# A decoder layer on one core: softmax joining in PSUM, weightings by table, filler transposes, new places

## The chip, the cores and the metric

The kernel runs on one core of one Trainium2 chip. The metric is device time in microseconds, from runs of the whole program; lower is better. The engines are TensorE (PE, with its weight loads PEld), VectorE (DVE), ScalarE (ACT), GpSimd (POOL) and SyncE (SP, which here issues most DMAs).

## The reference

One decoder layer over 1024 tokens of width 1024, in float32. The normalised input goes through one projection into 256 pooling channels and queries, keys and values for 12 heads of 64. Attention is evaluated under three (window, dilation) settings, merged by their softmax denominators.

```python
DILATED_CONFIGS = ((128, 1), (512, 4), (2048, 16))
def dilated_attention(q, k, v):
    for window, dilation in DILATED_CONFIGS:
        o, lse = dilated_branch(q, k, v, window, dilation)   # banded softmax; lse = m + log(den)
        ...
    w = softmax(stack(lses), axis=0)
    return sum(w[..., None] * stack(outs), axis=0)
...
h = rms_norm(x, ln_pre_mix); proj = h @ w_in
mix = concat([pool_out, attn_out]) @ w_out
x = x + rms_norm(mix, ln_post_mix)
h = rms_norm(x, ln_pre_ffn)
f = (silu(h @ w_gate) * (h @ w_up)) @ w_down
x = x + rms_norm(f, ln_post_ffn)
```

## The kernel before, in words

Each float32 product is three passes of TensorE: operands are split into a high part (ACT copies it) and a low part (DVE or POOL subtracts), and high x high, high x low and low x high are summed in PSUM. `wtile` loads a weight tile through the SP queue and splits it (line 245 is ACT's copy, line 249 the subtraction on POOL or DVE). `PRM['we']` says for each of the 12 query and key weight tiles whether DVE (1) or POOL (0) subtracts.

Attention is worked in 12 units, numbered 0 to 11. A unit is a pair of heads and a half of the tokens: pairs 0 to 3 with both halves, then pairs 4 and 5 in the first half (units 8 and 9) and in the second (10 and 11). A unit has five sorts of steps:

- `scores`: products of queries and keys into a bank of tag s; DVE adds the mask and takes the extremum (line 678), ACT takes the exponential and its sum (line 681). The result `pp` is not yet normalised. There are two sides: natural order and strided by four, which together cover the three settings.
- `merge`: the two sides' extrema and sums (`sx`) are joined into one weight per row, `wv`. Two small products (`ex` with a selector) bring the other side's numbers into a bank `e` of tag s; then some small steps follow on DVE, and one exponential on ACT: `em` (line 703), a reduction (704), the minimum `nm` (708), the difference `dd` (710), its exponential (711), `de` (713), the sum (714), the reciprocal (715) and `wv` (717).
- `weigh`: 16 pieces of `pp`, of 128 x 256 or 128 x 128, are multiplied by `wv` in place, by DVE (line 731) or POOL (line 733). One list `wd` of 16 entries says which, the same for all units. Pieces 0 to 3 are those of the first group.
- `values`, turning: groups of three or four blocks of `pp` are transposed through TensorE (line 197) into a bank of tag t; ACT copies the high part (778), DVE subtracts the low part (779), giving `ptr`.
- `values`, products: `ptr` times the values into a bank of tag o.

Beside these run the projections of the next pairs: rope on queries and keys (`rope`, whose two later steps at lines 453 and 456 are on POOL), and value rows. These projections are the "fill": lists of single products, cut into pieces, one piece to a unit.

Every step has a place on a common axis, in units, from `PRM`: `own` gives places for a single unit (`s0`, `s1` first and last score step, `m` merge, `w0`, `w1` weightings, `t0`, `t1` turnings, `v0`, `v1` products), `vt` the loads of values, `lr` and `lc` the loads of the mix for the output projection. `emit` sorts all steps by place and issues them; TensorE keeps the order in which its instructions are issued. Before a step that would wait, `await_` may pull products of the fill ahead: as many as the planner's own clock (0.235 us a product) says are needed before a due time, and `PRM["x"]` adds a number of further pulls for single steps. A negative number there takes the due time back by as many pulls.

After attention come the output projection, a norm, and the feed-forward part in blocks (a Strassen-like scheme of seven products instead of eight: `seven`, with sums of blocks at lines 1346 to 1352 on DVE, splits at 1380 and 1382 on ACT and POOL). `c0`, `c1` and `c2` hold the places of the norm's steps, squares and block sums in the passage from the one to the other, `ew` those of two weight loads.

Of the kernel before, what the change touches and what calls it, by code (L numbers as in the profile page):

```python
# [8 lines left out]
F32 = mybir.dt.float32  # L9
# [26 lines left out]
 'we': (1, 1, 1, 0, 0, 0, 0, 0, 0, 0, 1, 1),  # L36
 'nt0': 0.4926,
 'nt1': 0.628,
# [111 lines left out]
 'cut': 5,  # L150
 'ew': (0.2207, 0.1793),
 'c1': (0.1405, 0.1771, 0.2651, 0.7788, 0.6483, 1.0204, 1.4605, 1.6658, 0.9644, 0.8869),
 'c2': ((1.0107, 1.1787), (1.1914, 1.4876)),
 'e0': ((0.26, 0), (0.42, 0), (0.47, 0.9)),
 'ea': (0, 2, 4),
 'e1': (1.12, 1.25, 1.8, 1.2, 1.5)}
PRM["x"] = {(0, 'm'): 5, (0, 's', 0): 8, (0, 's', 1): 6, (0, 's', 2): 5, (0, 's', 3): 3, (0, 's', 4): 2, (0, 's', 6): 3,
# [31 lines left out]
def hybrid_block(ctx: ExitStack, tc: tile.TileContext, xT, w_in, w_v, w_pin, w_pool, w_out, w_gate, w_up, w_down,  # L189
# [27 lines left out]
    def bank(tag):  # L217
        return psum.tile([P, 512], F32, name="ps_" + tag, tag=tag)
# [226 lines left out]
    def eng(name):  # L445
        return [(nc.vector if b else nc.gpsimd) for b in PRM[name]]
# [107 lines left out]
    def new_q(pr, h):  # L554
        pr.q[h] = qkp.tile([P, 2, 512], F32R, name="qh", tag="qh", bufs=QB), qlow[len(taken) % 2]
        taken.append((pr.p, h))
        return pr.q[h]

    def q_half(pr, h):
        return proj_half(2 * pr.p, h, pr.st, lambda ps: rope(ps, h, new_q(pr, h), False, eng("rq")))  # L560

    def k_half(pr, h):
        def done(ps):
            if h == 0:
                pr.k = qkp.tile([P, 2, T], F32R, name="k", tag="k", bufs=2)
            did(("k", pr.p, h))
            rope(ps, h, pr.k, True, eng("rk"))
        return proj_half(2 * pr.p + 1, h, pr.st, done)
# [117 lines left out]
    def merge(pr, h):  # L686
# [20 lines left out]
        nm = small.tile([P, 16], F32, name="nm", tag="nm", bufs=1)  # L707
        nc.vector.tensor_tensor(nm, sv[:, 0, :, 0], sv[:, 1, :, 0], ALU.min)
        dd = small.tile([P, 2, 16], F32, name="dd", tag="dd", bufs=1)
        nc.vector.tensor_tensor(dd, nm[:, None].to_broadcast([P, 2, 16]), sv[:, :, :, 0], ALU.subtract)  # L710
# [3 lines left out]
        nc.vector.tensor_tensor(nm, de[:, 0], de[:, 1], ALU.add)
        nc.vector.reciprocal(nm, nm)
        wv = small.tile([P, 2, 4, 2], F32, name="wv", tag="wv")
        nc.vector.tensor_tensor(wv.rearrange("p s j a -> p (s j a)"), nm, dd[:, 0], ALU.mult)  # L717
# [4 lines left out]
    def weigh(pr, h):  # L722
        un = pr.un[h]

        def step(hd, side, j):
            un.wv
            did(("w", pr.p, h, hd, side))
            lo = 128 if narrow(side, h, j) else 0
            pv = un.pp[hd, side][:, j, lo:]
            if PRM["wd"][hd * 8 + (1 - side) * 4 + j]:  # L730
                nc.vector.tensor_scalar(pv, pv, un.wv[:, side, j, hd:hd + 1], None, op0=ALU.mult)
            else:
                nc.gpsimd.tensor_scalar(pv, pv, un.wv[:, side, j, hd:hd + 1], 1.0, op0=ALU.mult, op1=ALU.mult)  # L733
        return [lambda a=(hd, side, j): step(*a) for hd in range(2) for side in (1, 0) for j in range(4)]
# [26 lines left out]
    def values(pr, h):  # L761
# [5 lines left out]
        def turn(hd, gi):  # L767
# [187 lines left out]
    def put(steps, lo, hi):  # L955
        plan.append((steps, lo, hi))
# [833 lines left out]
```

## Time and profile before

| | |
|---|---|
| median of 3 runs | 1144.0 us (1143.02 to 1144.89) |
| profiled execution | 1144.5 us, span 1142.7 us |
| PE busy | 1126.4 us, 99% |
| DVE, ACT, POOL busy | 784.2, 545.3, 601.6 us |
| mean granted clock of PE | 0.997 |

In the profile's rows a time is that from the span's start, then the duration (of a run of like instructions, from the first's start to the last's end), the engine, the line of the kernel, the operation and the tiles. In brackets stands the idle time before it and the instruction that ended it. A line is often a helper's: line 194 is every product, line 197 every transpose.

### The profile page before, as it was taken

How to read it: one execution, taken by the hardware profiler on the slowest of the kernel's cores; microseconds unless marked ns; L12 is line 12 of the kernel's file. 1: busy time of each engine (PE TensorE's matmuls, PEld its weight loads, DVE VectorE, ACT ScalarE, POOL GpSimd, SP SyncE). 2: the span in 40 equal slices, each digit the busy share in tenths (PEclk: the TensorE clock that was granted, in tenths of full speed). 3: DMA queues.
4: the chain of work that ended last, by engine and by line, in shares of the span. 5: the costliest groups of instructions: out<-in, count | busy, mean ns of one | idle time of the engine just before them, and what ended most of it. 6: DMA issues, size and time to landing. Idle time of an engine off the chain costs nothing.

```text
span 1142.7 us, 17021 instructions
## 1 busy us (share of the span) xinstructions
PE 1126.4 (99%) x6050; PEld 976.5 (85%) x6050; DVE 784.2 (69%) x1463; ACT 545.3 (48%) x1035; POOL 601.6 (53%) x541
## 2 busy tenths in 40 slices
PE   9999999999999999999999999999999999999997
PEld 7999899999898888888788888888888888888887
DVE  7957878787898676979557655666566375464594
ACT  7446676666676665855333222322232435343431
POOL 0102646465576222241587556876675977656531
PEclk9999999999999999999999999999999999999999
DMA  8324151514136557530343354445445869766642
GB/s 286 114 79 167 56 167 57 166 57 166 57 111 225 187 203 272 184 111 28 129 175 141 127 195 174 166 175 196 173 149 191 286 207 364 230 206 200 203 166 73
DMA packets 85076, 189.02 MB, mean 165 GB/s; under 512 B 8704, under 2 KB 23552, under 8 KB 83584
## 3 DMA queue, kind: packets, MB, share of 16 engines
q1 hardware_dynamic: 84704, 187.68, 46.7%
q8 instruction: 47, 0.77, 0.3%
q14 instruction: 37, 0.30, 0.1%
q10 hardware_dynamic: 288, 0.27, 0.1%
HBM read 134.96 MB, written 52.95 MB: 164 GB/s over the span
## 4 chain that ended last, share of the span: by engine, by line
PE 83%; DVE 7%; POOL 3%; issue 3%; ACT 2%; DMA 1%; SPq 0%; DVEq 0%; POOLq 0%; ACTq 0%
PE ps_pj L194 29%; PE ps_o L194 22%; PE ps_s L194 21%; PE ps_t L194 7%; PE ps_t L197 3%; ACT pp L681 1%; DVE pp L678 1%; DVE sq L1137 1%; POOL fw L1382 1%; POOL whl L1382 1%; DMA xraw<-in_xT_dram 1%; POOL whl L249 0%; DVE z L1169 0%; DVE ql L484 0%; DMA rw<-in_w_up_dram 0%
## 5 line engine op out<-in xcount | busy, mean ns | idle before, releaser
L194 PE MATMUL ps_pj<-x,whl 128*128 128x512 f32 x480 | 141.7, 407 | 0.0
L1382 POOL TENSOR_TENSOR fw<-rw,fw 128x512 fp32r<-128x512 f32 x74 | 101.1, 1390 | 63.2 <-ACT fw L1380 61.8
L249 POOL TENSOR_TENSOR whl<-wraw,whl 128x512 fp32r<-128x512 f32 x50 | 66.4, 1348 | 110.3 <-ACT whl L245 110.2
L194 PE MATMUL ps_o<-tT,fw 128*128 128x512 f32 x504 | 119.4, 393 | 1.8 <-DVE p L1417 1.8
L194 PEld LDWEIGHTS ps_o<-tT,fw 128*128 128x128 f32 x504 | 95.5, 190 | 22.2 <-DVE p L1417 2.2
L733 POOL TENSOR_SCALAR pp<-pp,wv 128x256 f32<-128x256 f32 (+1 forms) x156 | 71.8, 480 | 80.1 <-DVE wv L717 71.4
L681 ACT ACTIVATE pp<-pp,sx 128x128 f32<-128x128 f32 (+1 forms) x192 | 89.4, 468 | 35.0 <-DVE sx L678 34.1
L1382 POOL TENSOR_TENSOR whl<-rw,whl 128x512 fp32r<-128x512 f32 x42 | 59.4, 1438 | 66.8 <-ACT whl L1380 66.8
L194 PEld LDWEIGHTS ps_pj<-x,whl 128*128 128x128 f32 x480 | 84.9, 189 | 9.2
L1380 ACT ACTIVATE fw<-rw 128x1024 fp32r<-128x1024 f32 x37 | 38.5, 1056 | 94.5 <-DVE rw L1348 41.3
L194 PE MATMUL ps_pj<-whl,x 128*128 128x256 f32 x528 | 80.9, 293 | 0.0
L1529 POOL TENSOR_TENSOR op<-rw,op 128x512 fp32r<-128x512 f32 x38 | 60.4, 1588 | 36.3 <-ACT op L1528 36.2
L1528 ACT ACTIVATE op<-rw 128x1024 fp32r<-128x1024 f32 x38 | 40.2, 1060 | 65.9 <-DMA rw<-bd 25.5
L194 PEld LDWEIGHTS ps_pj<-whl,x 128*128 128x128 f32 x528 | 70.3, 196 | 0.1
L779 DVE TENSOR_TENSOR ptr<-ps_t,ptr 128x512 fp32r<-128x512 f32 (+1 forms) x84 | 55.8, 665 | 14.3 <-ACT ptr L778 13.9
L194 PE MATMUL ps_pj<-b,fw 128*128 128x512 f32 x264 | 61.6, 389 | 0.0
L453 POOL TENSOR_TENSOR rsw<-rsw,sinr 128x512 f32<-128x512 f32 x20 | 26.3, 1317 | 66.4 <-DVE rsw L451 66.4
L194 PE MATMUL ps_o<-ptr,v 128*128 128x128 f32 (+1 forms) x472 | 56.5, 254 | 1.9 <-DVE ptr L779 1.2
L194 PEld LDWEIGHTS ps_pj<-b,fw 128*128 128x128 f32 x264 | 49.5, 188 | 10.3
L778 ACT ACTIVATE ptr<-ps_t 128x512 fp32r<-128x512 f32 (+1 forms) x84 | 48.4, 576 | 20.3 <-PE ps_t L197 18.9
L194 PEld LDWEIGHTS ps_o<-ptr,v 128*128 128x128 f32 x472 | 52.6, 163 | 5.7 <-DVE ptr L779 1.6
L194 PE MATMUL ps_s<-k,qh 128*128 128x128 f32 (+1 forms) x192 | 53.7, 291 | 0.0
(318 smaller groups left out, 2897.9 us busy)
## 6 DMA issues: line engine op xcount, KB each, us to landing
rw<-bd SPq DMA_DIRECT2D x77, 256.0 KB, 4.5
v<-vd SPq DMA_DIRECT2D x22, 512.0 KB, 4.8
rw<-wsd SPq DMA_DIRECT2D x44, 256.0 KB, 3.9
rw<-in_w_gate_dram SPq DMA_DIRECT2D x20, 512.0 KB, 3.7
rw<-in_w_up_dram SPq DMA_DIRECT2D x20, 512.0 KB, 4.6
bd<-p SPq DMA_DIRECT2D x33, 256.0 KB, 3.0
rw<-in_w_down_dram SPq DMA_DIRECT2D x33, 256.0 KB, 4.3
fw<-in_w_down_dram SPq DMA_DIRECT2D x16, 512.0 KB, 4.1
```

Source lines behind the costliest of these rows:

```text
L194: return tc.keep_in_program_order(nc.tensor.matmul(*a, **k))
L197: return tc.keep_in_program_order(nc.tensor.transpose(dst, src, by))
L249: parts.append(eng.tensor_tensor(dst[:, 1, at:at + w], src[:, at:at + w], dst[:, 0, at:at + w].bitcast(F32), ALU.subtract))
L453: pin(eng[0].tensor_tensor(s, s, sinr[:, sl], ALU.mult))
L681: nc.scalar.activation(pt[:, j, lo:], pt[:, j, lo:], AF.Exp, bias=sx[:, 0, side, j, hd, 0:1], scale=-1.0, accum_out=sx[:, 0, side, j, hd, ...
L733: nc.gpsimd.tensor_scalar(pv, pv, un.wv[:, side, j, hd:hd + 1], 1.0, op0=ALU.mult, op1=ALU.mult)
L778: nc.scalar.activation(ptr[:, 0, :w], t[:, :w], AF.Copy)
L779: nc.vector.tensor_tensor(ptr[:, 1, :w], t[:, :w], ptr[:, 0, :w].bitcast(F32), ALU.subtract)
L1380: nc.scalar.activation(w[n][:, :, 0], raw[n], AF.Copy)
L1382: low[0] = nc.gpsimd.tensor_tensor(w[n][:, i, 1], raw[n][:, i], w[n][:, i, 0].bitcast(F32), ALU.subtract)
L1528: nc.scalar.activation(w[:, :, 0], raw, AF.Copy)
L1529: nc.gpsimd.tensor_tensor(w[:, 0, 1], raw[:, 0], w[:, 0, 0].bitcast(F32), ALU.subtract)
```

## The change

- `merge`: `nm` and `dd` are put into the free columns of the PSUM bank `e` instead of SBUF; the minimum and the sum become reductions over two rows; the sum and reciprocal go into a new small tile `ns`.
- `weigh`: a table `wu`, by unit and piece, overrides `wd`; the value 2 is ACT, as a copy scaled by the column of `wv`.
- `turn`: a table `dm`, by unit and group, gives a number of transposes of the identity into the group's bank ahead of its own; it holds one entry, 18 for group 0 of unit 9.
- `eng`: a table `ro` overrides the engines of a rope step; one of its ten entries differs from the default (pair 2's key, second half, addition on DVE).
- the fill's borders between units are moved by `fb`, in threes of products.
- `we`: other weight tiles are split on DVE.
- places (`own`, `vt`, `lr`, `lc`, `c0`, `c1`, `c2` and others) and the numbers of further pulls (`x`) are changed.

```diff
- 'we': (1, 1, 1, 0, 0, 0, 0, 0, 0, 0, 1, 1),
+ 'we': (0, 0, 0, 1, 1, 0, 0, 1, 0, 1, 0, 1),
- 'lw': (4.153, 0.453),
+ 'lw': (4.665, 0.499),
...
          9: {'s0': -0.058,
-             't1': 1.7709,
+             't1': 1.7717,
              'v1': 2.0469,
-             'w1': 1.052,
-             'w0': 0.6506,
-             'v0': 1.2034,
-             's1': 0.464,
-             't0': 0.9223,
-             'm': 0.6239},
+             'w1': 1.0264,
+             'w0': 0.6547,
+             'v0': 1.1793,
+             's1': 0.4719,
+             't0': 0.8982,
+             'm': 0.6222},
...
          6: {'s1': 0.3673,
...
+             'w1': 1.2338,
+             's0': -0.0707,
+             'w0': 0.6079,
+             't0': 0.8477},
...
- 'c0': (0.0502, 0.0986, 0.2259, 0.595, 0.2709, 0.6103, -0.3497, 0.3883, 0.2606, 0.1296),
+ 'c0': (0.0502, 0.0986, 0.2259, 0.595, 0.2709, 0.6103, -0.3497, 0.3883, 0.1363, 0.1661),
- 'ew': (0.2207, 0.1793),
- 'c1': (0.1405, 0.1771, 0.2651, 0.7788, 0.6483, 1.0204, 1.4605, 1.6658, 0.9644, 0.8869),
- 'c2': ((1.0107, 1.1787), (1.1914, 1.4876)),
+ 'ew': (0.2363, 0.1483),
+ 'c1': (0.1405, 0.1771, 0.2651, 0.7788, 0.5274, 0.9613, 1.4605, 1.6658, 0.9644, 0.9565),
+ 'c2': ((1.0107, 1.1699), (1.1914, 1.6904)),
...
+ 'wu': {(8, 7): 1, (6, 10): 2, ...  (9, 1): 2, (9, 6): 2, (9, 7): 2, (9, 9): 2, (7, 0): 2, (7, 1): 2, (7, 7): 2, ...
+        (4, 2): 2, (4, 3): 2, (4, 4): 2, (4, 11): 2, (4, 12): 2, (4, 14): 2, (4, 15): 2, ...},
+ 'dm': {(9, 0): 18},
+ 'fb': (1, 0, 0, 0, 0, 0, 1, -1, 0),
+ 'ro': {..., ('rk', (2, 1)): (0, 1), ...}}
...
-    def eng(name):
-        return [(nc.vector if b else nc.gpsimd) for b in PRM[name]]
+    def eng(name, key=None):
+        return [(nc.vector if b else nc.gpsimd) for b in G["ro"].get((name, key), G[name])]
...
-        nm = small.tile([P, 16], F32, name="nm", tag="nm", bufs=1)
-        nc.vector.tensor_tensor(nm, sv[:, 0, :, 0], sv[:, 1, :, 0], ALU.min)
-        dd = small.tile([P, 2, 16], F32, name="dd", tag="dd", bufs=1)
+        nm, dd = e[:, 128:144], e[:, 160:192].rearrange("p (o n) -> p o n", o=2)
+        de = small.tile([P, 64], F32, name="de", tag="de", bufs=1)[:, :32].rearrange("p (o n) -> p o n", o=2)
+        ns = small.tile([P, 16], F32, name="ns", tag="ns", bufs=1)
+        nc.vector.tensor_reduce(nm, sv[:, :, :, 0].rearrange("p o n -> p n o"), op=ALU.min, axis=mybir.AxisListType.X)
         nc.vector.tensor_tensor(dd, nm[:, None].to_broadcast([P, 2, 16]), sv[:, :, :, 0], ALU.subtract)
         nc.scalar.activation(dd, dd, AF.Exp)
-        de = small.tile([P, 2, 16], F32, name="de", tag="de", bufs=1)
         nc.vector.tensor_tensor(de, dd, sv[:, :, :, 1], ALU.mult)
-        nc.vector.tensor_tensor(nm, de[:, 0], de[:, 1], ALU.add)
-        nc.vector.reciprocal(nm, nm)
+        nc.vector.tensor_reduce(ns, de.rearrange("p o n -> p n o"), op=ALU.add, axis=mybir.AxisListType.X)
+        nc.vector.reciprocal(ns, ns)
         wv = small.tile([P, 2, 4, 2], F32, name="wv", tag="wv")
-        nc.vector.tensor_tensor(wv.rearrange("p s j a -> p (s j a)"), nm, dd[:, 0], ALU.mult)
+        nc.vector.tensor_tensor(wv.rearrange("p s j a -> p (s j a)"), ns, dd[:, 0], ALU.mult)
...
-            if PRM["wd"][hd * 8 + (1 - side) * 4 + j]:
+            n = hd * 8 + (1 - side) * 4 + j
+            e = G["wu"].get((unit_of[pr.p, h], n), G["wd"][n])
+            if e == 2:
+                nc.scalar.activation(pv, pv, AF.Copy, scale=un.wv[:, side, j, hd:hd + 1])
+            elif e:
                 nc.vector.tensor_scalar(pv, pv, un.wv[:, side, j, hd:hd + 1], None, op0=ALU.mult)
...
             t = bank("t")
+            for n in range(G["dm"].get((unit_of[pr.p, h], hd * len(groups) + gi), 0)):
+                turned_to(t[:, :P], idt, idt)
...
+    seq, ends_at = [x for fs in fill for f in fs for x in f], [0]
     for u in range(1, 11):
-        put(Fill([x for f in fill[u] for x in f]).by(3), u + (G["f0"] if u > 1 else -0.07), u + (0.25 if u == 10 else 1) + G["f1"])
+        ends_at.append(sum(len(f) for fs in fill[:u + 1] for f in fs) + (3 * G["fb"][u - 1] if u < 10 else 0))
+    for u in range(1, 11):
+        put(Fill(seq[ends_at[u - 1]:ends_at[u]]).by(3), u + (G["f0"] if u > 1 else -0.07), u + (0.25 if u == 10 else 1) + G["f1"])
```

More of the change, by code (lines that the diff above doesn't have):

```diff
@@ L35 @@
  'sqa': (1, 0, 0, 1, 0, 0, 0, 1),
- 'we': (1, 1, 1, 0, 0, 0, 0, 0, 0, 0, 1, 1),
- 'nt0': 0.4926,
- 'nt1': 0.628,
+ 'we': (0, 0, 0, 1, 1, 0, 0, 1, 0, 1, 0, 1),
+ 'nt0': 0.5548,
+ 'nt1': 0.5715,
  'oq': (0, 1, 1, 1, 0, 0, 0, 1),
@@ L41 @@
  'fl': 12,
[2 rows of a table removed]
+ 'lt': 2.711,
+ 'ls': 2.296,
  'lm': 2.745,
[4 rows of a table removed]
+ 'lw': (4.665, 0.499),
+ 'nm': 0.1243,
+ 'n2': -0.0696,
+ 'n0': 0.1888,
  'n1': 0.223,
@@ L71 @@
         'u3': 0.5838},
[7 rows of a table removed]
+ 'f0': -0.0347,
+ 'f1': 0.0016,
+ 'own': {0: {'s0': 0.5606,
+             's1': 0.7789,
+             'm': 0.7979,
+             'w0': 1.0202,
+             'w1': 1.211,
              't0': 1.1072,
              'v0': 1.259,
[4 rows of a table removed]
+             'v1': 1.9554,
+             't1': 1.8552},
+         11: {'w1': 1.0918, 't1': 1.4526, 'v1': 1.9549, 's1': 0.549, 'w0': 0.8029, 's0': -0.0018, 'm': 0.7619},
+         4: {'m': 0.7092,
+             'w0': 0.7447,
+             'w1': 1.247,
+             't1': 1.7615,
+             'v0': 1.3849,
+             'v1': 2.0002,
+             's1': 0.4549,
+             's0': 0.0229},
+         8: {'t1': 1.7658,
+             'w1': 0.8402,
+             'v0': 1.1586,
+             's1': 0.5108,
+             'w0': 0.6677,
+             'v1': 1.7393,
+             'm': 0.612,
+             's0': -0.0747,
+             't0': 0.8029},
          9: {'s0': -0.058,
[1 row of a table removed]
+             't1': 1.7717,
              'v1': 2.0469,
[7 rows of a table removed]
+             'w1': 1.0264,
[4 more added lines that the diff above has]
+             'm': 0.6222},
+         3: {'s0': -0.0954,
              't1': 1.7965,
@@ L97 @@
              'v0': 1.1127,
[1 row of a table removed]
+             's1': 0.6,
              'w1': 1.5434,
[1 row of a table removed]
+             'm': 0.6192,
              'v1': 2.0031},
[1 row of a table removed]
+         1: {'t0': 0.9112,
              'w0': 0.7327,
[1 row of a table removed]
+             'v0': 1.1094,
              'w1': 1.2937,
@@ L108 @@
              's0': 0.0051,
[3 rows of a table removed]
+             's1': 0.5555,
+             'v1': 1.9757},
+         10: {'t1': 1.4978,
+              't0': 0.9959,
+              'v1': 1.9807,
+              's1': 0.5578,
+              'w1': 1.104,
+              'v0': 1.103,
+              'w0': 0.677,
+              's0': 0.0309},
+         6: {'s1': 0.3673,
              't1': 1.9214,
[1 row of a table removed]
+             'v0': 1.2396,
              'v1': 2.0149,
[1 row of a table removed]
+             'w1': 1.2338,
              'm': 0.5559,
[4 rows of a table removed]
+             's0': -0.0707,
+             'w0': 0.6079,
+             't0': 0.8477},
+         7: {'w0': 0.7712,
+             't1': 1.8573,
              'm': 0.6559,
@@ L123 @@
              's1': 0.4937,
[1 row of a table removed]
+             'v1': 2.0474,
              'v0': 1.1321,
[1 row of a table removed]
+             'w1': 1.4422,
              's0': 0.0043},
[3 rows of a table removed]
+         5: {'s1': 0.644,
+             'v1': 2.0727,
+             'w1': 1.3558,
+             'w0': 0.701,
+             'v0': 1.0974,
+             'm': 0.6212,
+             't1': 1.9059,
+             's0': -0.0126},
+         2: {'t1': 1.8275, 'm': 0.5677, 'w0': 0.7538, 's0': 0.0264, 'v1': 1.9978, 'w1': 1.0366}},
+ 'vt': ((1.029, 1.2775), (2.7383, 3.2018), (4.97, 5.5237), (6.9389, 7.4289), (8.9599, 10.3692), (9.9449, 10.1116)),
  'pw': 0.4464,
[1 row of a table removed]
+ 'pm': (0.8885, (0.7589, 0, 0), (0.84, 1, 0), (1.0163, 0, 1), (1.0616, 1, 1)),
  'rq': (0, 0),
@@ L139 @@
  'wd': (0, 1, 1, 0, 0, 0, 0, 0, 0, 0, 1, 0, 0, 0, 0, 0),
[4 rows of a table removed]
+ 'lr': (9.7769, 9.8146, 9.9709, 10.2193),
+ 'lw0': (9.8897, 10.3805),
+ 'lc': (11.9989, 12.0997, 11.939, 12.182),
+ 'o0': 10.4939,
  'o1': 11.122,
[5 rows of a table removed]
+ 'o2': 12.6657,
+ 'np': 11.7112,
+ 'z0': 12.3784,
+ 'z1': 13.8875,
+ 'c0': (0.0502, 0.0986, 0.2259, 0.595, 0.2709, 0.6103, -0.3497, 0.3883, 0.1363, 0.1661),
  'cut': 5,
- 'ew': (0.2207, 0.1793),
- 'c1': (0.1405, 0.1771, 0.2651, 0.7788, 0.6483, 1.0204, 1.4605, 1.6658, 0.9644, 0.8869),
- 'c2': ((1.0107, 1.1787), (1.1914, 1.4876)),
+ 'ew': (0.2363, 0.1483),
@@ L154 @@
+ 'c1': (0.1405, 0.1771, 0.2651, 0.7788, 0.5274, 0.9613, 1.4605, 1.6658, 0.9644, 0.9565),
+ 'c2': ((1.0107, 1.1699), (1.1914, 1.6904)),
  'e0': ((0.26, 0), (0.42, 0), (0.47, 0.9)),
  'ea': (0, 2, 4),
- 'e1': (1.12, 1.25, 1.8, 1.2, 1.5)}
-PRM["x"] = {(0, 'm'): 5, (0, 's', 0): 8, (0, 's', 1): 6, (0, 's', 2): 5, (0, 's', 3): 3, (0, 's', 4): 2, (0, 's', 6): 3,
[21 rows of a table removed]
+ 'e1': (1.12, 1.25, 1.8, 1.2, 1.5),
+ 'wu': {(8, 7): 1,
+        (6, 10): 2,
+        (6, 12): 0,
+        (9, 12): 0,
+        (10, 1): 1,
+        (6, 7): 0,
+        (0, 0): 0,
+        (8, 8): 1,
+        (10, 3): 2,
+        (0, 1): 0,
+        (0, 13): 2,
+        (8, 2): 2,
+        (8, 1): 2,
+        (4, 15): 2,
+        (4, 4): 2,
+        (8, 4): 2,
+        (10, 5): 2,
+        (5, 11): 2,
+        (4, 2): 2,
+        (4, 12): 2,
+        (4, 3): 2,
+        (9, 1): 2,
+        (10, 11): 1,
+        (10, 12): 2,
+        (7, 7): 2,
+        (7, 11): 1,
+        (10, 6): 1,
+        (10, 4): 2,
+        (5, 10): 2,
+        (10, 15): 0,
+        (1, 9): 0,
+        (9, 6): 2,
+        (2, 13): 2,
+        (2, 3): 2,
+        (4, 11): 2,
+        (2, 4): 1,
+        (2, 9): 2,
+        (2, 10): 0,
+        (2, 2): 2,
+        (8, 6): 0,
+        (10, 8): 1,
+        (9, 7): 2,
+        (9, 9): 2,
+        (8, 0): 0,
+        (8, 11): 0,
+        (7, 0): 2,
+        (7, 10): 1,
+        (7, 1): 2,
+        (1, 14): 0,
+        (8, 5): 0,
+        (8, 10): 2,
+        (8, 13): 2,
+        (0, 10): 2,
+        (6, 14): 1,
+        (0, 5): 0,
+        (1, 10): 1,
+        (10, 9): 0,
+        (4, 14): 2,
+        (11, 10): 2,
+        (11, 2): 2,
+        (1, 8): 2,
+        (11, 7): 0,
+        (3, 7): 2,
+        (11, 3): 2},
@@ new lines @@
+ 'dm': {(9, 0): 18},
+ 'fb': (1, 0, 0, 0, 0, 0, 1, -1, 0),
+ 'ro': {('rk', (1, 0)): (0, 0),
+        ('rq', (1, 0)): (0, 0),
+        ('rk', (3, 0)): (0, 0),
+        ('rk', (4, 0)): (0, 0),
+        ('rq', (2, 0)): (0, 0),
+        ('rk', (2, 1)): (0, 1),
+        ('rk', (5, 1)): (0, 0),
+        ('rq', (4, 1)): (0, 0),
+        ('rk', (1, 1)): (0, 0),
+        ('rq', (5, 1)): (0, 0)}}
+PRM["x"] = {(0, 'm'): 4, (0, 's', 0): 8, (0, 's', 1): 6, (0, 's', 2): 5, (0, 's', 3): 3, (0, 's', 4): 2, (0, 's', 6): 3,
[21 rows of a table added]
@@ L559, in q_half @@
     def q_half(pr, h):
-        return proj_half(2 * pr.p, h, pr.st, lambda ps: rope(ps, h, new_q(pr, h), False, eng("rq")))
+        return proj_half(2 * pr.p, h, pr.st, lambda ps: rope(ps, h, new_q(pr, h), False, eng("rq", (pr.p, h))))
     def k_half(pr, h):
@@ L566, in done @@
             did(("k", pr.p, h))
-            rope(ps, h, pr.k, True, eng("rk"))
+            rope(ps, h, pr.k, True, eng("rk", (pr.p, h)))
         return proj_half(2 * pr.p + 1, h, pr.st, done)
@@ L706, in merge @@
         sv = sx.rearrange("p o s j a b -> p o (s j a) b")
-        nm = small.tile([P, 16], F32, name="nm", tag="nm", bufs=1)
-        nc.vector.tensor_tensor(nm, sv[:, 0, :, 0], sv[:, 1, :, 0], ALU.min)
-        dd = small.tile([P, 2, 16], F32, name="dd", tag="dd", bufs=1)
+        nm, dd = e[:, 128:144], e[:, 160:192].rearrange("p (o n) -> p o n", o=2)
+        de = small.tile([P, 64], F32, name="de", tag="de", bufs=1)[:, :32].rearrange("p (o n) -> p o n", o=2)
+        ns = small.tile([P, 16], F32, name="ns", tag="ns", bufs=1)
+        nc.vector.tensor_reduce(nm, sv[:, :, :, 0].rearrange("p o n -> p n o"), op=ALU.min, axis=mybir.AxisListType.X)
         nc.vector.tensor_tensor(dd, nm[:, None].to_broadcast([P, 2, 16]), sv[:, :, :, 0], ALU.subtract)
         nc.scalar.activation(dd, dd, AF.Exp)
-        de = small.tile([P, 2, 16], F32, name="de", tag="de", bufs=1)
         nc.vector.tensor_tensor(de, dd, sv[:, :, :, 1], ALU.mult)
-        nc.vector.tensor_tensor(nm, de[:, 0], de[:, 1], ALU.add)
-        nc.vector.reciprocal(nm, nm)
+        nc.vector.tensor_reduce(ns, de.rearrange("p o n -> p n o"), op=ALU.add, axis=mybir.AxisListType.X)
+        nc.vector.reciprocal(ns, ns)
         wv = small.tile([P, 2, 4, 2], F32, name="wv", tag="wv")
-        nc.vector.tensor_tensor(wv.rearrange("p s j a -> p (s j a)"), nm, dd[:, 0], ALU.mult)
+        nc.vector.tensor_tensor(wv.rearrange("p s j a -> p (s j a)"), ns, dd[:, 0], ALU.mult)
+        for i in range(17):
+            due["w", pr.p, h, i] = clock[0] + G["lw"][0] + G["lw"][1] * i
         un.wv = wv
```

86 rows, old and new, of the table PRM are left out of this document.

## The prediction

> **What bounds the kernel now.** I read the head of the page, then the busy times by stretch, then the chain of waits that TensorE (PE) ended, and last the timeline around each of those waits.
>
> ```profile
> span 1142.7 us, 17021 instructions
> PE 1126.4 (99%) x6050; PEld 976.5 (85%) x6050; DVE 784.2 (69%) x1463; ACT 545.3 (48%) x1035; POOL 601.6 (53%) x541
> ```
>
> PE is busy for 1126.4 of 1142.7 us. Nothing in this change takes a product away, so only the 16.3 us in which PE stands still can be won, and what PE loses while its clock is low. The profiled execution took 1144.5 us, 0.5 over the median of 1144.0; I make the sum against the span and take it off the median.
>
> Stretches: length, busy us of PE, PEld, DVE, ACT and POOL, granted clock, DMA share, GB/s.
>
> ```profile
> 100.00:140.00 40.00, 39.27 (x263) 36.33 (x263) 33.53 (x99) 26.92 (x73) 21.68 (x25) 1.00 0.34 119
> 300.00:340.00 40.00, 37.97 (x255) 34.58 (x255) 35.12 (x109) 27.32 (x73) 27.62 (x39) 1.00 0.25 88
> 340.00:380.00 40.00, 37.50 (x256) 35.31 (x255) 33.99 (x98) 30.07 (x84) 22.20 (x25) 0.96 0.72 259
> 540.00:580.00 40.00, 38.23 (x163) 31.11 (x163) 23.55 (x30) 14.80 (x21) 25.91 (x21) 0.96 0.29 105
> 740.00:920.00 180.00, 180.00 (x796) 149.05 (x795) 104.15 (x119) 56.24 (x67) 133.15 (x98) 1.00 0.53 192
> ```
>
> The feed-forward part (740 to 920 stands for it) has no idle PE at all. The loss sits in attention and at one place of the passage into the feed-forward part, and in two stretches the clock was 0.96 as well: 4% of 40 us is 1.6 us each. The waits behind it, with total, number and longest:
>
> ```profile
> PE ps_t L197 <- POOL pp L733: 3.2, 3, 1.9
> PE ps_o L194 <- DVE p L1417: 1.8, 1, 1.8
> PE ps_o L194 <- DVE ptr L779: 1.2, 2, 0.8
> PE ps_o L194 <- ACT ptr L778: 0.7, 1, 0.7
> PE ps_s L194 <- DVE ex L697: 0.6, 1, 0.6
> ```
>
> The largest is the transposes (L197) waiting for the weightings on POOL (L733). Its worst case lies in unit 9 (pair 5, first half), group 0:
>
> ```profile
> 354.74 2.54 PE L194 MATMUL ps_pj<-whl,x 128*128 128x256 f32 x20
> 355.84 1.30 POOL L453 TENSOR_TENSOR rsw<-rsw,sinr 128x512 f32<-128x512 f32 x1 [6.72 <-DVE rsw L451]
> 356.18 0.99 DVE L714 TENSOR_TENSOR nm<-de 128x16 f32<-128x16 f32 x1
> 357.09 2.51 POOL L249 TENSOR_TENSOR whl<-wraw,whl 128x512 fp32r<-128x512 f32 x2
> 357.49 0.92 DVE L717 TENSOR_TENSOR wv<-nm,dd 128x16 f32<-128x16 f32 x1
> 359.58 0.72 POOL L733 TENSOR_SCALAR pp<-pp,wv 128x128 f32<-128x128 f32 x2
> 360.01 0.82 PE L197 MATMUL ps_t<-idt,pp 128*128 128x128 f32 x4 [1.86 <-POOL pp L733]
> 360.48 3.86 PE L194 MATMUL ps_pj<-whl,x 128*128 128x256 f32 x18
> ```
>
> Two things make this wait. The weights wv end at 358.41, and POOL is still in a weight split (L249) until 359.60. After it 18 products of 128x256 take 3.86 us, 0.214 each, where the 20 before took 0.127 each: 18 x 0.087 = 1.6 us lost to the clock, as the stretch says.
>
> **The change part by part.**
>
> *18 transposes of the identity ahead of unit 9's group 0.* They need the identity and a free ps_t bank, not the weightings, so they run where PE waits.
>
> ```profile
> 388.69 0.60 PE L197 MATMUL ps_t<-idt,pp 128*128 128x128 f32 x4
> L197 PE MATMUL ps_t<-idt,pp 128*128 128x128 f32 x144 | 22.9, 278 | 3.3 <-POOL pp L733 3.2
> ```
>
> Four in a row take 0.60 us and one 0.278, so starts are (0.60 - 0.278)/3 = 0.107 apart: 18 take 1.93 us, at most 18 x 0.15 = 2.7. I take 1.95, against 1.86 us of wait: +0.1. If they keep PE from standing still, the clock drop goes: -1.6. Were the weightings early and the wait gone by itself, the 1.95 would be paid in full, but 1.86 of wait and 1.6 of clock would be gone too, so this part alone gives about -1.5 either way.
>
> Here a page speaks against me. No run of more than four transposes stands in this trace, so it cannot say whether transposes hold the clock. The Trainium skill, "TensorE: Matmul & The Clock Gate", Part 4, says that a transpose does not count as PE-busy in the same way and doesn't bring the full clock; by that rule the drop stays and this part is +0.1 instead of -1.5.
>
> *Joining steps in PSUM.* Per merge (12 of them) a minimum (L708) and an addition (L714) of two inputs become reductions of one, and the exponent's tile dd and the minimum nm go to the PSUM bank e. Durations min/median/max:
>
> ```profile
> L703 DVE TENSOR_TENSOR em<-ps_s,qdA x12: 204/210/225, 88.8 to 413.4; 128x64 f32<-128x64 f32 x12
> L710 DVE TENSOR_TENSOR dd<-nm,sx x12: 176/192/745, 89.8 to 416.4; 128x32 f32<-128x32 f32 x12
> L714 DVE TENSOR_TENSOR nm<-de x12: 168/175/991, 93.2 to 419.9; 128x16 f32<-128x16 f32 x12
> L717 DVE TENSOR_TENSOR wv<-nm,dd x12: 160/174/920, 93.7 to 420.3; 128x16 f32<-128x16 f32 x12
> ```
>
> L703, the one with a PSUM input, never stretches (225 at most), while those with two inputs in SBUF go to 0.75 to 0.99 us when POOL runs beside them (L714 at 356.18 under POOL's L453, L717 under L249). The new steps have at most one SBUF input each, so I expect about 0.2 us for each of them everywhere. In unit 9 this brings wv forward by 0.82 + 0.75 = 1.57 us, but there POOL's split ends last, so it is worth nothing for POOL's weightings. L710's stretch falls where no PE wait is recorded. Bounds: -0.8 (half of unit 9's) to +0.3 (a little more for each of the smaller steps in the few places where PE waits); I take -0.2.
>
> The bank e is now held until wv is written. PE can be stopped only by the second request for an s bank after it. The tightest place:
>
> ```profile
> 237.61 0.18 DVE L717 TENSOR_TENSOR wv<-nm,dd 128x16 f32<-128x16 f32 x1
> 242.00 0.22 PE L194 MATMUL ps_s<-k,qh 128*128 128x128 f32 x1
> ```
>
> That leaves 4.2 us: nothing.
>
> *Weightings by table.* Counting the table over 12 units x 16: POOL 156 to 125, DVE 36 to 30, ACT 0 to 37.
>
> ```profile
> L733 POOL TENSOR_SCALAR pp<-pp,wv x156: 365/476/1438, 94.0 to 427.3; 128x256 f32<-128x256 f32 x114, 128x128 f32<-128x128 f32 x42
> L681 ACT ACTIVATE pp<-pp,sx 128x128 f32<-128x128 f32 x60 | 23.6, 396 | 18.8 <-DVE sx L678 18.6
> L590 ACT ACTIVATE vs<-ps_pj,n1r 128x256 fp32r<-128x256 f32 x20 | 8.4, 470 | 7.5 <-PE ps_pj L194 5.6 <-DMA vd<-vs 1.7
> ```
>
> POOL loses 31 x 0.46 = 14 us. No row shows ACT weighting; the nearest (L590, a copy scaled by a column, and the narrow L681) give 0.40 to 0.47, so ACT gains about 37 x 0.45 = 17 us over ten and more windows in which it has 10 to 13 of 40 us free. PE sees only what stands before a group. In unit 7 one piece of group 0 leaves POOL and one DVE, both for ACT; in unit 9 one leaves DVE; unit 1's first four do not change.
>
> ```profile
> 123.37 0.81 PE L197 MATMUL ps_t<-idt,pp 128*128 128x128 f32 x4 [0.73 <-POOL pp L733]
> 303.44 0.81 PE L197 MATMUL ps_t<-idt,pp 128*128 128x128 f32 x4 [0.58 <-POOL pp L733]
> ```
>
> Unit 7's 0.58 shrinks by about one weighting, 0.4; unit 1's stays. Bounds -1.3 (both go) to +6, if ACT's queue stands still behind a weighting (the second rival). I take -0.4.
>
> *Splits, ropes, fill borders.* Counting w_in loads (tiles 8 and 10 are loaded twice), DVE splits 5 instead of 4 and POOL one fewer; one rope addition goes from POOL to DVE; two borders of the fill move by three products.
>
> ```profile
> L249 POOL TENSOR_TENSOR whl<-wraw,whl 128x512 fp32r<-128x512 f32 x50 | 66.4, 1348 | 110.3 <-ACT whl L245 110.2
> L249 DVE TENSOR_TENSOR whl<-wraw,whl 128x1024 fp32r<-128x1024 f32 x15 | 20.7, 1381 | 4.2 <-ACT whl L245 4.0
> ```
>
> POOL -2.7 us, DVE +1.4 us; POOL's 110 us of idle before L249 cover the one, DVE's 5 to 6.5 us free in each 40 the other. Without that cover a late split is 1.4 us of PE. Zero.
>
> *Places asked anew.* About a hundred small moves of steps, vector loads and DMA issues with them, of 0.01 to 0.3 of a unit, and changed counts of products pulled ahead (0.235 each in the planner). They meet the remaining attention waits: 0.73 in unit 1 (one pull more before its group 0), 0.66 and 0.79 in unit 6's last product:
>
> ```profile
> 300.74 0.38 PE L194 MATMUL ps_o<-ptr,v 128*128 128x256 f32 x1 [0.66 <-ACT ptr L778]
> ```
>
> and 0.6 at unit 10's merge; 2.8 together. The SP queue's loads move by under a third of a unit (about 9 us); none of the attention waits above was ended by a DMA. Bounds -2.8 (all go) to +2.8 (as much again opens elsewhere). The pulls are added just at these places, so I take half: -1.4.
>
> *Passage into the feed-forward part.* Squares earlier, the last block sums and their splits later.
>
> ```profile
> 564.52 1.86 DVE L1346 TENSOR_TENSOR wraw<-rw 128x1024 f32<-128x1024 f32 x1 [2.64 <-DMA rw<-in_w_up_dram]
> 566.91 0.67 DVE L1417 TENSOR_TENSOR p<-ps_o,sq 128x512 f32<-128x512 f32 x1
> 567.64 4.61 PE L194 MATMUL ps_o<-tT,fw 128*128 128x512 f32 x12 [1.77 <-DVE p L1417]
> ```
>
> PE waits for an eviction that is queued on DVE behind a sum which waited for a weight load. The moved steps lie 20 to 30 us before; whether POOL's splits, which free that load's room, begin earlier, no row says. Bounds: -3.4 (wait 1.77 and clock 1.6 go) to +1.8 (as long again). I take 0.
>
> Sum: +0.1 - 1.6 - 0.2 - 0.4 + 0 - 1.4 + 0 = -3.5; 1144.0 - 3.5 = 1140.5 us.
>
> **The rivals.** *The clock drop stays*, because a run of transposes does not hold the clock or because another gap brings the drop. For it: nothing here shows a long run of transposes. Against: the trace lists a transpose as a MATMUL of 128x128 like any other. 1140.5 + 1.6 = 1142.1.
>
> *ACT blocks the evictions: slower.* ACT is in order. A weighting issued before wv is there holds the copies of transposed groups (L778) behind it, and PE's next products. Place: units with three and more ACT weightings (2, 4, 7, 8, 9, 10, 11). For it: in unit 9 the last steps up to wv alone took from 356.18 to 358.41, and one late copy (L778) already cost 0.66. Against: so far the copies wait for PE, 16.8 us in all:
>
> ```profile
> L778 ACT ACTIVATE ptr<-ps_t 128x512 fp32r<-128x512 f32 x72 | 42.5, 591 | 18.1 <-PE ps_t L197 16.8 <-PE ps_o L194 0.7
> ```
>  At 0.85 us (unit 6's waits were 0.66 and 0.79) in each of seven units it is 6 us: 1146.5. It decides from 0.83 us in each of the seven, where 3.5 us of gain turn into 2.3 of loss.
>
> *The new places only shift the waits*: without the -1.4 and -0.4, 1142.3.
>
> *The passage is freed too*: DVE's sum gets its load 2 us sooner; -3.4: 1137.1.
>
> **How the numbers follow.** Forecast 0.42, drop stays 0.13, places only shift 0.16, ACT blocks 0.15, passage freed 0.14. A measurement of this kernel tells about 0.2%, 2.3 us, from no change: faster is under 1141.7, slower over 1146.3. Faster: 0.42 + 0.14 + 0.04 (the better ends of the two middle cases) = 0.60; slower: 0.12 of the ACT case; same: the rest, 0.28. The range leaves out the better half of the freed passage and the worst of the ACT case: 1136.5 to 1146.0. The forecast's own is 1138.5 to 1141.7.
>
> **What would show it.** Right: 18 transposes in a row just before unit 9's group 0, no 1.86 us wait there, clock 1.00 in that stretch; no joining step over 0.3 us; 37 weightings of 0.4 to 0.5 us on ACT; PE idle in attention down by about 2 us beyond that. Wrong: a clock of 0.96 still in that stretch; PE waits on ACT's L778 in several units; the wait of 1.77 us at the passage gone, or a new one beside it.

## The result, and the profile after

The changed kernel took 1137.66 us (median of 6 runs, 1136.9 to 1139.92), the kernel before 1143.65 in the same comparison. The ratio is 0.9949 (95% interval 0.9937 to 0.9962): 5.8 us less by the ratio, where 3.5 was forecast. The head of its page:

```profile
span 1136.0 us, 17063 instructions
PE 1124.2 (99%) x6068; PEld 976.1 (86%) x6068; DVE 785.5 (69%) x1459; ACT 556.7 (49%) x1072; POOL 585.9 (52%) x507
```

The span is 6.7 us shorter. PE's 18 further transposes are in it. Its waits (engine, line, releaser, total, number, longest):

```profile
PE ps_o L302 <- DVE p L1536: 1.5, 1, 1.5
PE ps_s L302 <- DVE ex L805: 1.0, 1, 1.0
PE ps_o L302 <- DVE ptr L895: 0.4, 1, 0.4
```

Lines have moved: L1536 was L1417, L895 was L779, L847 (POOL's weighting) was L733. In attention the waits for weightings, 3.2 us, are gone altogether; those for `ptr` fell from 1.9 to 0.4, and only the one at unit 10's merge grew, from 0.6 to 1.0. The one at the passage fell from 1.8 to 1.5. The last line of the table of stretches, for the 400 us of attention from 60 to 460 us, first before, then after:

```profile
sum 400.00, PE 393.95 PEld 362.17 DVE 306.34 ACT 260.02 POOL 187.19; mean PE 39.39 PEld 36.22 DVE 30.63 ACT 26.00 POOL 18.72
```

```profile
sum 400.00, PE 398.50 PEld 367.19 DVE 308.70 ACT 276.18 POOL 170.65; mean PE 39.85 PEld 36.72 DVE 30.87 ACT 27.62 POOL 17.07
```

PE stands still for 1.5 us there instead of 6.05. POOL has 16.5 us less to do, ACT 16 more. Three of the stretches shown before (length, busy times, clock, DMA share, GB/s):

```profile
300.00:340.00 40.00, 40.00 (x277) 37.31 (x276) 34.17 (x103) 31.25 (x84) 28.65 (x33) 1.00 0.30 97
340.00:380.00 40.00, 39.02 (x269) 36.27 (x268) 32.93 (x106) 30.55 (x84) 20.15 (x25) 1.00 0.80 287
540.00:580.00 40.00, 38.47 (x172) 31.50 (x172) 24.97 (x30) 14.70 (x19) 27.73 (x21) 1.00 0.31 116
```

The clock is 1.00 in both places where it was 0.96. Unit 9's group 0 in the timeline:

```profile
352.19 2.54 POOL L357 TENSOR_TENSOR whl<-wraw,whl 128x512 fp32r<-128x512 f32 x2
354.30 0.17 DVE L825 TENSOR_TENSOR wv<-ns,ps_s 128x16 f32<-128x16 f32 x1
354.32 2.15 PE L305 MATMUL ps_t<-idt 128*128 128x128 f32 x18
354.69 1.28 POOL L564 TENSOR_TENSOR rco<-rco,rsw 128x512 f32<-128x512 f32 x1
355.89 1.48 ACT L843 ACTIVATE pp<-pp,wv 128x128 f32<-128x128 f32 x4
355.94 4.22 POOL L847 TENSOR_SCALAR pp<-pp,wv 128x128 f32<-128x128 f32 x8
356.37 0.67 PE L305 MATMUL ps_t<-idt,pp 128*128 128x128 f32 x4
356.80 3.12 PE L302 MATMUL ps_pj<-whl,x 128*128 128x256 f32 x24
```

The 18 transposes start 0.15 us before wv is written and end at 356.47. POOL is not free for its pieces when wv is there (354.47): the split lasts until 354.73, and a rope step (L564) until 355.97. The 24 products behind them take 0.13 us each: full clock. The joining's steps (min/median/max in ns):

```profile
L819 DVE TENSOR_TENSOR ps_s<-ps_s,sx x12: 179/199/200, 83.9 to 412.1; 128x32 f32<-128x32 f32 x12
L822 DVE TENSOR_REDUCE ns<-de x12: 169/188/191, 86.1 to 416.0; 128x16 f32<-128x32 f32 x12
L825 DVE TENSOR_TENSOR wv<-ns,ps_s x12: 160/170/173, 86.6 to 416.4; 128x16 f32<-128x16 f32 x12
L843 ACT ACTIVATE pp<-pp,wv x37: 387/492/512, 87.2 to 417.5; 128x256 f32<-128x256 f32 x21, 128x128 f32<-128x128 f32 x16
```

None of the steps that the change touches is over 0.21 us now. `ex`, which it left with two inputs in SBUF, still goes up to 1.30 us (L805 at 196.66). ACT's weightings have means of 0.39 and 0.50 us by width, against 0.40 and 0.47 in the nearest rows, and no wait of PE in attention was ended by ACT.

### The profile page after: what moved, and what is told of

It is laid out like the page before. It is cut to its first block, busy times and chain, and to the rows that moved or that the text cites. A ratio compares the mean times of both kernels' runs of the same rounds, so it can differ in the third digit from the quotient of the medians.

```text
span 1136.0 us, 17063 instructions
## 1 busy us (share of the span) xinstructions
PE 1124.2 (99%) x6068; PEld 976.1 (86%) x6068; DVE 785.5 (69%) x1459; ACT 556.7 (49%) x1072; POOL 585.9 (52%) x507
## 4 chain that ended last, share of the span: by engine, by line
PE 87%; DVE 5%; issue 2%; POOL 2%; ACT 2%; DMA 1%; SPq 0%; DVEq 0%; POOLq 0%
PE ps_pj L302 32%; PE ps_o L302 23%; PE ps_s L302 22%; PE ps_t L302 7%; PE ps_t L305 3%; DVE sq L1256 1%; POOL fw L1501 1%; ACT pp L789 1%; DMA xraw<-in_xT_dram 1%; POOL whl L1501 1%; DVE z L1288 0%; DMA rw<-in_w_up_dram 0%; DVE z L1289 0%; DVE z L1416 0%; DMA wraw<-in_w_gate_dram 0%
## 5 line engine op out<-in xcount | busy, mean ns | idle before, releaser
L847 POOL TENSOR_SCALAR pp<-pp,wv 128x256 f32<-128x256 f32 (+1 forms) x125 | 59.4, 498 | 130.0 <-issue 51.9
L895 DVE TENSOR_TENSOR ptr<-ps_t,ptr 128x512 fp32r<-128x512 f32 (+1 forms) x84 | 55.8, 666 | 16.7 <-ACT ptr L894 16.3
```

The source lines that it names most:

```text
L895: nc.vector.tensor_tensor(ptr[:, 1, :w], t[:, :w], ptr[:, 0, :w].bitcast(F32), ALU.subtract)
```

## The experiments

Each was timed against the kernel before, whose median was 1142.9 us in the first four, 1143.2 in the next four and 1142.5 in the last four. "After" is the changed kernel. Since the median of before differs by up to 1.2 us between these rounds, kernels of different rounds are compared by their ratios to before.

### The transposes alone, away, and doubled

Edits: the loop with 18 put into the kernel before; in after, `'dm': {}` and `'dm': {(9, 0): 36}`.

> The kernel before with only the 18 transposes added. Theory (a run of transposes holds the clock): no wait over 0.3 us ahead of the group, clock 1.0 in that stretch, 1143.7 - 1.5 = about 1142.2 us. Rival (transposes do not count for the clock): 18 transposes stand in the wait, the clock is still at half for 3.4 us after them, 1143.7 us.

> The changed kernel without its 18 transposes of the identity. Theory (the transposes take the place of a wait of PE and so keep its clock): PE waits about 2.0 us for the weightings ahead of unit 9's group 0, the clock is at half for 3.4 us after it, and the time is 1137.7 + 1.6 - 0.1 = about 1139.2 us. Rival (the new places and earlier weights would have removed the wait anyway): no wait over 0.5 us there, clock 1.0 in that stretch, and the time falls by the transposes' 1.9 us, to about 1135.8 us.

> The changed kernel with 36 transposes of the identity instead of 18 ahead of unit 9's group 0. Theory (18 just fill the wait): 18 more cost their full 18 x 0.11 = 2.0 us, about 1139.7 us, clock 1.0 in that stretch. Rival (the wait is longer than the 18, so some of the further ones are covered too): under 1 us more, under 1138.7 us.

Before with the transposes: 1141.97 us, ratio 0.9992 (0.9983 to 1.0001). Its timeline and its stretch:

```profile
358.03 2.13 PE L197 MATMUL ps_t<-idt 128*128 128x128 f32 x18
360.50 2.39 PE L194 MATMUL ps_pj<-whl,x 128*128 128x256 f32 x18
340.00:380.00 40.00, 39.33 (x279) 36.77 (x279) 35.29 (x102) 30.53 (x84) 22.31 (x25) 1.00 0.72 259
```

The same 18 products that took 3.86 us take 2.39: in this profile the mechanism is as told, 1.47 us. In the median only 0.9 is seen, at the edge of what can be told from nothing.

After without them: 1138.13 us, ratio 0.9953 (0.9941 to 0.9966), 0.5 us over the changed kernel by the ratios, which these intervals do not tell apart. Its wait and stretch:

```profile
PE ps_t L305 <- POOL pp L847: 1.9, 1, 1.9
340.00:380.00 40.00, 38.13 (x249) 35.48 (x249) 32.41 (x105) 30.24 (x85) 19.68 (x24) 0.96 0.81 284
```

The wait and the drop are back, so the rival (the wait would be gone anyway) falls. One profile could be chance, since the drop does not follow every such wait, but all seven profiles with transposes there and no longer wait than 0.9 us behind them have the clock at 1.00 in this stretch; of the six without the transposes, five have the drop. (An eighth with them, that with the old splits below, has a wait of 2.5 us behind them, and the drop.)

After with 36: 1141.43 us, ratio 0.9986 (0.9977 to 0.9995), some 4 us more than after, where 2.0 was expected.

```profile
354.10 4.12 PE L305 MATMUL ps_t<-idt 128*128 128x128 f32 x36
340.00:380.00 40.00, 39.25 (x278) 36.83 (x278) 31.70 (x102) 29.73 (x83) 18.80 (x23) 1.00 0.79 283
PE ps_o L302 <- DVE p L1536: 2.8, 1, 2.8
540.00:580.00 40.00, 37.20 (x160) 30.30 (x159) 23.29 (x29) 14.73 (x20) 24.70 (x20) 0.96 0.30 105
```

The further 18 cost 1.97 us (4.12 - 2.15) and nothing covers them: that is the theory's 2.0. The rest comes from elsewhere: the passage's wait is 1.3 us longer in this profile, and there the clock drops. Why the shift lengthens that wait was not tried.

### The joining, the table and the places, singly and together

Edits: in before, the joining of the change (`b_psum`); in after, the joining of before (`a_sbuf`); `'wu': {}` (`a_no_wu`); all three away, joining, table and transposes (`b_places`); table and transposes away (`places_psum`). "Places" below is all that is then left of the change: places, pulls, splits' engines, the fill's borders, the rope step and the passage.

> The kernel before with only the joining's small steps moved into the PSUM bank. Theory (one SBUF input each, so POOL does not hold them up, but PE's worst wait ends with POOL's weight split): no joining step over 0.3 us, unit 9's wait of 1.9 us stays, 1143.7 - 0.2 = about 1143.4 us. Rival (the weights' lateness sets the wait): unit 9's wait falls by 1.5 us and its clock drop goes, about 1140.6 us.

> The changed kernel with the joining back in SBUF, without the table of weightings and without the 18 transposes: what is left of the change is the places, the numbers of pulls, the fill's borders, the splits' engines and the passage. Theory (the places remove most of the waits by themselves): PE's waits in attention fall from 5.7 us to under 3.5 us, about 1140.0 us. Rival (the places only fit together with the table and the PSUM steps): waits as before or longer, 1143 us or more.

> The changed kernel without the table of weightings and without the 18 transposes: the places and the joining in PSUM together. Each alone gave 0 to 1.0 us. Theory (the places ask for the groups at times that only the shorter joining meets): the two together give 4 us and more, about 1138.8 us, with a wait of about 2 us ahead of unit 9's group 0 left. Rival (the gains simply add, and the table and the transposes hold the rest): 1 us, about 1142 us, waits of 4 us and more in attention.

> The changed kernel with only the joining's small steps back in SBUF. Theory (they decide nothing where PE waits): joining steps of 0.7 to 1.0 us appear again under POOL's two-input work, the time grows by under 1 us, to about 1138.2 us. Rival (the places count on the earlier weights): waits for weightings of 1 us and more in several units, 1140 us or more.

> The changed kernel without the table of weightings: 156 pieces on POOL, 36 on DVE, none on ACT. Theory (the third engine shortens what stands before a group): the transposes wait for POOL again, 1 to 2 us in all, about 1139.2 us. Rival (POOL had room, and ACT pays for it): no more wait than in the changed kernel, 1137.7 us or a little less.

Measured:

| kernel | median us | ratio to before (95%) | PE idle, 60 to 460 us |
|---|---|---|---|
| before | 1142.5 to 1143.65 | 1 | 6.05 |
| before + joining in PSUM | 1143.15 | 1.0001 (0.9992 to 1.001) | 5.82 |
| before + places | 1142.21 | 0.9992 (0.9983 to 1.0001) | 5.29 |
| before + places + joining | 1139.5 | 0.9966 (0.9954 to 0.9978) | 3.03 |
| + table (after without transposes) | 1138.13 | 0.9953 (0.9941 to 0.9966) | 2.39 |
| + transposes (after) | 1137.66 | 0.9949 (0.9937 to 0.9962) | 1.50 |
| after, joining in SBUF | 1139.96 | 0.997 (0.9958 to 0.9981) | 2.74 |
| after, no table | 1138.29 | 0.9953 (0.9939 to 0.9966) | 1.07 |

The last column is 400 us less PE's busy time in one profile of each.

Joining and places give nothing that can be told from noise when alone, and 0.34% together. PE's idle time says the same: 0.2 and 0.8 us less alone, 3.0 together. So the places alone did neither what the theory expected (1140.0 us) nor what the rival did (1143 us or more), and together they came near the theory's 1138.8. About half of the 2 us that the two save only together lies ahead of unit 9's group 0, where the places alone make the wait 1.1 us longer and the joining takes that back; the rest is spread over smaller waits from 300 to 330 us. First the wait for POOL's weightings of before with the joining, then with the places, then with both:

```profile
PE ps_t L197 <- POOL pp L735: 3.3, 3, 1.8
```

```profile
PE ps_t L242 <- POOL pp L782: 3.4, 3, 2.9
```

```profile
PE ps_t L242 <- POOL pp L784: 1.9, 1, 1.9
```

With the old places the earlier wv is worth nothing, since POOL's split ends last (with the joining in PSUM, wv at 357.53 and the split at 360.29). With the new places POOL has the split and a rope step of 1.3 us (L501) ahead of the weightings. With the places alone, then with both:

```profile
355.92 1.23 DVE L755 TENSOR_TENSOR dd<-nm,sx 128x32 f32<-128x32 f32 x1
357.05 1.28 POOL L501 TENSOR_TENSOR rco<-rco,rsw 128x512 f32<-128x512 f32 x1
358.91 0.17 DVE L762 TENSOR_TENSOR wv<-nm,dd 128x16 f32<-128x16 f32 x1
359.18 4.48 POOL L782 TENSOR_SCALAR pp<-pp,wv 128x128 f32<-128x128 f32 x8 [0.86 <-DVE wv L762]
```

```profile
354.69 0.17 DVE L762 TENSOR_TENSOR wv<-ns,ps_s 128x16 f32<-128x16 f32 x1
355.36 1.26 POOL L501 TENSOR_TENSOR rco<-rco,rsw 128x512 f32<-128x512 f32 x1
356.61 3.53 POOL L784 TENSOR_SCALAR pp<-pp,wv 128x128 f32<-128x128 f32 x7
```

In SBUF the steps stretch beside POOL (`dd` to 1.23 us), wv comes last, and POOL stands idle 0.86 us for it; in PSUM wv is there 1.75 us before POOL is free. PE waits 2.9 us in the one and 1.9 in the other. The same in after with the joining in SBUF, a step of it, and the timeline:

```profile
L818 DVE TENSOR_TENSOR dd<-nm,sx x12: 173/194/1234, 83.9 to 414.1; 128x32 f32<-128x32 f32 x12
356.37 2.15 PE L305 MATMUL ps_t<-idt 128*128 128x128 f32 x18
358.61 0.17 DVE L825 TENSOR_TENSOR wv<-nm,dd 128x16 f32<-128x16 f32 x1
359.39 0.68 PE L305 MATMUL ps_t<-idt,pp 128*128 128x128 f32 x4 [0.86 <-POOL pp L845]
```

Here wv ends 2.4 us after PE begins its transposes, not 0.15 as in after, and PE waits 0.86 us behind all 18. Its time, 1139.96, lies by the rival (1140) and not by the theory (1138.2), though no wait for weightings is over 0.9 us. The table's worth is between 0.5 us (after against after without it) and 1.5 (the two rows with and without it where no transposes stand); neither step is clear of its intervals, and in the first PE's idle time is not less with the table (1.50) than without (1.07). In the kernel without the table the transposes did not wait for POOL, so the expected 1 to 2 us fell away: with the transposes in front POOL has the time.

### The splits, the fill's borders and the ropes undone

```diff
- 'we': (0, 0, 0, 1, 1, 0, 0, 1, 0, 1, 0, 1),
+ 'we': (1, 1, 1, 0, 0, 0, 0, 0, 0, 0, 1, 1),
- 'fb': (1, 0, 0, 0, 0, 0, 1, -1, 0),   'ro': {...}
+ 'fb': (0, 0, 0, 0, 0, 0, 0, 0, 0),    'ro': {}
```

> The changed kernel with the weight splits' engines, the fill's borders and the rope's engine as before. Theory (POOL and DVE have room for the splits, so they decide nothing by themselves): 1137.7 us within 0.8. Rival (the splits' engines set when POOL comes to the weightings ahead of a group): waits for POOL of 1 us and more again, 1139.5 us or more.

1151.1 us, ratio 1.0078 (1.0061 to 1.0095): 13 to 15 us slower than after (by the medians, by the ratios), and 0.8% slower than before. Its six runs stand in two groups, three at 1149.1 to 1149.2 and three at 1153.0 to 1154.4; the profile is of 1149.1. Three of its waits, unit 9's group 0, and the stretch around it:

```profile
PE ps_t L296 <- POOL pp L838: 2.8, 2, 2.5
PE ps_o L293 <- DVE ptr L886: 2.4, 2, 1.9
PE ps_s L293 <- DVE sx L777: 1.6, 1, 1.6
```

```profile
359.79 0.17 DVE L816 TENSOR_TENSOR wv<-ns,ps_s 128x16 f32<-128x16 f32 x1
361.00 2.49 POOL L348 TENSOR_TENSOR whl<-wraw,whl 128x512 fp32r<-128x512 f32 x2
364.06 0.85 PE L296 MATMUL ps_t<-idt,pp 128*128 128x128 f32 x4 [2.53 <-POOL pp L838]
340.00:380.00 40.00, 35.81 (x249) 34.08 (x248) 30.04 (x93) 28.34 (x77) 18.72 (x21) 0.91 0.73 254
```

A weight split has come between wv and POOL's weightings: 2.49 us on POOL, 2.53 on PE, in spite of the transposes. The rival is right. In this profile PE stands still for 8.8 us between 60 and 460 us (busy 391.18 of 400), 7.3 more than in after, and the clock of 0.91 costs about 9% of 40 us, 3.6 us: together nearly all of the 11.3 us between the two spans. What makes the upper group slower still is open, and which of the three (splits, borders, rope) does most was not separated.

### The passage

Edits: `c0`, `c1`, `c2` and `ew` as before (`a_passage_b`); and, in both kernels, DVE's three block sums of the first later block issued only behind the eviction that PE waits for:

```diff
             if n[0] == "S" and "S3" not in raw:
-                block_sums()
+                with tc.issue_after(taken7[0].ins) if j == EARLY // 2 + 1 else ExitStack():
+                    block_sums()
```

> The changed kernel with the four lists of the passage into the feed-forward part as before. Theory (the passage's places gave nothing; its clock drop comes and goes by itself from run to run): the wait there is 1.5 to 1.8 us as before, 1137.7 us within 0.6. Rival (the moved squares and splits freed it): the wait grows by 0.5 us and more and the clock drops behind it in most runs, 1139.5 us or more.

> The kernel before, with DVE's three block sums of the first later block put behind the last eviction that PE waits for in the passage. Theory (that eviction is ready at 563 us and is held on DVE by a sum that waits for a weight load): the wait of 1.8 us at 566 us goes, the clock drop behind it too where it was there, about 1143.2 - 1.8 - 0.8 = 1140.6 us. Rival (the products behind it then wait for the weights that the sums make): the wait moves some 6 us on and the time stays at 1143 us.

> The changed kernel, with DVE's three block sums of the first later block put behind the last eviction that PE waits for in the passage. Theory: its wait of 1.5 us goes and with it the clock drop that follows it in some runs, about 1135.7 us. Rival (the products behind it wait for the later sums): 1137.7 us.

With the old lists: 1137.33 us, ratio 0.9947 (0.9933 to 0.996), the wait 1.7 us. The moved squares and splits gave nothing that can be told from noise. With the sums put later, before took 1142.17 (0.9996, 0.9987 to 1.0004) and after 1136.04 (0.9943, 0.9931 to 0.9955). The wait is gone from the stretch in both; here after's:

```profile
540.00:580.00 40.00, 40.00 (x180) 33.14 (x179) 26.84 (x30) 14.71 (x19) 28.64 (x21) 1.00 0.37 132
```

In before PE has no such wait later on either, so it has not moved as the rival says; but the time fell by 0.3 us (median) to 0.5 us (ratio) only, where the theory said 1140.6 us. Why the time does not follow the wait is open. In after the wait stands one block later, from the same cause:

```profile
595.85 1.23 DVE L1465 TENSOR_TENSOR wraw<-rw 128x1024 f32<-128x1024 f32 x1 [9.62 <-DMA rw<-in_w_up_dram]
597.00 0.68 DVE L1537 TENSOR_TENSOR sq<-ps_o,q 128x512 f32<-128x512 f32 x1
597.82 2.52 PE L302 MATMUL ps_o<-tT,fw 128*128 128x512 f32 x10 [1.50 <-DVE sq L1537]
```

DVE waits 9.6 us for a weight load with an eviction queued behind it. So the cause of the passage's wait is shown, but not that its removal shortens the run: by the ratios after gains 0.7 us, within the intervals, and this version, the lowest median of all, is not shown to beat after.

## Why the prediction was right or wrong

The time lies in the range, and PE's waits in attention went as told: PE stands still 4.55 us less there, 1.86 of it unit 9's wait. The size was too small, 3.5 against 5.8. Put in one after another, places and joining measured 3.9, the table 1.5 and the transposes 0.5, and only the first is clear of its interval; the forecast had 1.6, 0.4 and 1.5 for them. A transposes' term that was too large made up for part of the others, and that is luck. The time itself, 1137.66, is nearest to the rival of the freed passage (1137.1), but that rival did not happen: the passage's wait is still 1.5 us. The terms failed mainly because I added parts that only work together.

- *Transposes (+0.1 and -1.6).* Right in place and mechanism: 18 in the wait, 0.119 us each with the last one's end (2.15 us; the sum's 1.95 left that end out), clock 1.00 behind them. Their worth in the median is 0.5 to 0.9 us, not 1.5, and not clear of noise: the drop that they prevent does not come in every run. The rival that the drop stays is refuted. (The trace of before did have longer runs of transposes than four: six in a row at 1129 us.) The Trainium skill, "TensorE: Matmul & The Clock Gate", Part 4, says that a transpose does not count as PE-busy in the same way and does not bring the full clock; here 18 in 2.15 us (after) and even 36 in 4.12 us (after with 36), ahead of the rest, left the clock at 1.00 in the stretch 340 to 380 us, so for these float32 transposes the measurement decides against it as to keeping a full clock. Whether they would raise a lowered one, no run here shows.
- *Joining (-0.2) and places (-1.4).* This is the step that failed. Alone they measured 0.0 and about -0.9; together -0.34%, some 3.9 us. My sentence that in unit 9 the earlier wv "is worth nothing for POOL's weightings" was true of the old places alone. With the new ones POOL is through with its split and its rope step before a wv worked out in SBUF is there, and then the joining in PSUM is worth 2 to 3 us in all.
- *Stretch.* Right for the steps moved: 0.21 us at most with one SBUF input, up to 1.23 with two, in after with the joining in SBUF. The Trainium skill, "GPSIMD Engine Reference", 1. Specifications, says that POOL shares its SBUF interfaces with VectorE and contends with DVE instructions of two SBUF inputs; the trace agrees, 0.17 us becoming 0.92 (L717) in before and 0.17 at most after (L825).
- *Table (-0.4).* Between -0.5 and -1.5, not resolved. ACT did not block the evictions, so the slower rival falls.
- *Splits, ropes, borders (0).* As a term this was wrong: I priced the engine time that moves and let idle time cover it, but a split of 2.5 us in POOL's order decides by what stands behind it. Undone, the three together cost 13 to 15 us with the new places, and one wait of 2.5 us is shown to come from such a split; with the old places they were not tried. (Three borders of the fill move, not two.)
- *Passage (0).* Right in the median. In the two profiles it looks like 1.8 us of gain (0.2 of wait, 1.6 of clock), but the lists have no part in it that shows: without them the clock there is 1.00 too.

## What to carry to other kernels

Here POOL's start was set by the last of several things (its own queue, or wv), so price a part by what ends last once the other parts are in, not in the old schedule; two parts that each measure nothing can be worth 4 us together. Look for the long instruction ahead of the one that is waited for (a split on POOL, a sum on DVE that waits for a load), since here its place counted for more than its engine's load. A clock drop in one profile is not a term of the median.

## What the runs showed of the hardware

The clock drop behind a wait of PE comes and goes. Inside the kernel it lasted 3.41 us each time, at half clock (0.50); in before:

```profile
360.39:363.80 3.41, 3.41 (x18) 3.41 (x17) 2.68 (x5) 2.33 (x4) 3.41 (x7) 0.50 0.97 337
```

Waits of 1.8 to 2.9 us ahead of unit 9's group 0 were followed by it in six profiles (in one of them with the transposes in front) and not in one (before with the sums later, clock 1.00 from 340 to 380 us, with a drop at 303 us instead); waits of 1.4 to 1.8 us at the passage were followed by it in one profile and not in ten. In after with the old splits a wait of 1.9 us at 202 us was not followed by it, and one of 1.6 at 375 us was, so the length of a wait alone does not decide. It shows in the runs of before: 22 with a mean clock of 0.999 averaged 1142.5 us, 9 with 0.996 averaged 1144.9.

ACT's exponential of 128 x 32 took 0.23 us in SBUF and 0.18 in PSUM:

```profile
L711 ACT ACTIVATE dd<-dd x12: 219/229/233, 91.6 to 417.9; 128x32 f32<-128x32 f32 x12
```

```profile
L820 ACT ACTIVATE ps_s<-ps_s x12: 173/182/207, 85.1 to 413.9; 128x32 f32<-128x32 f32 x12
```
